# Moving the operand sums of the first product group ahead, next to the norm's operands, in a two-layer hybrid encoder

## The chip, the cores and the metric

The kernel runs on one core of one Trainium2 chip. The metric is device time in microseconds (us): the median of several executions of the whole program. One more execution is taken with the hardware profiler, and all views of the profile are of that one. The engines are called as in the profile: PE (matrix multiply) with PEld (its weight loads), DVE (vector), ACT (scalar and activation functions), POOL (GpSimd) and SP (which here only issues DMAs).

## The reference

The program is an encoder trunk of two layers on 256 tokens of width 1024, in float32. Per layer there are two SwiGLU blocks of inner width 2816 and an attention mixer between them; the edit concerns the SwiGLU blocks.

```
for l in range(DEPTH):
    x = x + 0.5 * swiglu(rms_norm(x, ffn1_norm[l]), ffn1_w_gate[l], ffn1_w_up[l], ffn1_w_down[l])
    h = rms_norm(x, mix_norm[l])
    ...                                   # projection, windowed and differential attention
    x = x + jnp.concatenate([out_a, out_b], axis=-1) @ w_out[l]
    x = x + 0.5 * swiglu(rms_norm(x, ffn2_norm[l]), ffn2_w_gate[l], ffn2_w_up[l], ffn2_w_down[l])
return rms_norm(x, final_norm)

def swiglu(h, w_gate, w_up, w_down):
    return (jax.nn.silu(h @ w_gate) * (h @ w_up)) @ w_down
```

## The kernel before

**Precision.** Every matrix is split into a high part, which ACT casts to the fast matmul type, and a low part, which DVE gets by subtracting the high part from the original. A product is three matmuls: high by high, low by high, high by low. So every weight of the network passes through ACT once (the cast) and DVE once (the subtraction). In the profile these are `CAST w<-raw` and `TENSOR_TENSOR w<-raw,w`, each on half of a raw tile (128x1024).

**Weights.** A raw tile is 1 MB of weights. There are six slots for raw tiles (`N_RAW`). SP loads a tile into a slot as soon as the slot's last reader, a subtraction on DVE, is done. `weights()` (line 249) hands out the next tile and calls `ahead` (line 228), which emits the splits in order, up to `look[0]` half tiles ahead of use. With `less` the call looks less far ahead.

**A SwiGLU block** (`ffn`, line 600) works through the inner width in groups of 512 columns, 0 to 4, and a rest of 256. Group 0 is computed plainly: gate and up (`gs`, `us`) over eight chunks of the inner dimension, in two passes of four (`tokens`). Then ACT computes the silu of the gate (`gate`, the activation `tmp<-ps,r`), and DVE multiplies it with up (`hidden`, the operation `s<-ps,hr,tmp`, one per token half). The hidden values are transposed by PE (`turn`, matmuls `ps<-ident,s`), split, and multiplied with the down weights in the next group.

**Groups of seven products.** For the groups in `SEVEN` gate and up are computed together by `by_seven` (line 632), a Strassen-like scheme: seven products of 512x512 weight quarters instead of eight. In the first block of layer 0 these are groups 2 to 4; in the other three blocks they are groups 1 to 4. Per group there are four raw tiles: a and d (quarters of gate), b and c (quarters of up). A DMA issued by POOL gathers c onto b (tile b+c), another gathers b onto a (tile a+b), and DVE adds c and then d to a+b. Products 1, 2 and 4 use quarters of the normalised input; products 3, 7, 5 and 6 use four sums of these quarters. In group 1 the order on PE is: product 1, transposes of the first half of group 0's hidden values, product 2, transposes of the second half, first down tile of group 0, products 3, 7, 5, 6, 4, second down tile.

**The sums.** `Norm.copies` (line 339) has ACT make plain float32 copies of the transposed input out of PSUM: eight activations `s<-ps,gcol`. `Norm.make_sums` (line 349) is a generator: its first step adds the first two sums on DVE (`tmp<-s,s`), the second casts them on ACT (`q<-tmp`), the third takes their low parts and adds the other two sums, the fourth casts those (`q<-tmp`, `v<-tmp`), and the fifth takes their low parts. The caller steps it with `next(sums)`.

**Order.** PE, ACT, DVE and POOL execute their instructions in the order in which they are written here: in the SwiGLU blocks that order is kept (`Kept`, line 40). Each engine runs its own list and waits for semaphores of the others. An instruction that waits holds up all that stand behind it on its engine. PSUM has eight banks; a product can start only when a bank has been read out.

**Norm statistics.** `before(1)` makes the operands of the last four chunks and the last squares; `before(2)` has DVE sum the squares (`ms<-nss`), POOL take the power (`r<-ms,mhalf`), DVE halve the result (`hr<-r`), and then lets waiting gathers go to POOL's queue (`flush`).

Of the kernel before, what the change touches and what calls it, by code (L numbers as in the profile page):

```python
# [29 lines left out]
IN_FFN, IN_MIX = 8, 6  # L30
# [4 lines left out]
def trunk(ctx: ExitStack, tc: tile.TileContext, x, n1, g1, u1, d1, nm, w_in, sink,  # L35
# [35 lines left out]
    def bank():  # L71
        return ps.tile([P, 512], F32, tag="ps", bufs=8, name=nm_("ps"))

    def halves(b):
        return b.rearrange("p (a n) -> p a n", a=2)

    def blk(dt=F32R):
        return s4.tile([P, 2, 512], dt, tag="s4", name=nm_("s4"))

    def tmp(tag="tmp", bufs=5, shape=(P, 2, 256), dt=F32):  # L80
        return tp.tile(list(shape), dt, tag=tag, bufs=bufs, name=nm_(tag))
# [143 lines left out]
    look = [IN_MIX]  # L225
# [23 lines left out]
    def weights(less=0, held=False):  # L249

        i = at["use"]
        at["use"] += 1
        if i > 1:
            ahead(2 * i + look[0] - less)
        w = loaded[i]
        w.held = held
        return w
# [179 lines left out]
    norm = Norm(0)  # L437
# [101 lines left out]
    def split(dst, src, scale=None):  # L539

        act.copy(dst[:, :, 0:S], src)
        dve.tensor_tensor(dst[:, :, S:512], src, f(dst[:, :, 0:S]), op=ALU.subtract)
# [57 lines left out]
    def ffn(norm, aside=None, before=None, final=False, sevens=SEVEN[1]):  # L600
        def silu(out_, acc, t):
            act.activation(out_, acc, AF.Silu, scale=norm.r[:, t:t + 1])
            return out_

        def gate(gs):
            g = []
            for t in range(2):
                n = gs[t].shape[1]
                g.append(silu(tmp().rearrange("p a n -> p (a n)")[:, :n], gs[t], t))
            return g  # L610

        def up(h, acc, g, t):
            n = acc.shape[1]
            dve.scalar_tensor_tensor(h[:, t, :n], in0=acc, scalar=norm.hr[:, t:t + 1], in1=g, op0=ALU.mult, op1=ALU.mult)

        def hidden(g, us):
            h = blk(F32)
            for t in range(2):
                up(h, us[t], g[t], t)
            return h  # L620

        def prod(xo, w):
            acc = bank()
            for k in range(4):
                hi, lo = w.part(k)
                xh, xl = xo(k)
                pe.matmul(acc, lhsT=xh, rhs=hi, start=k == 0, stop=False)
                pe.matmul(acc, lhsT=xl, rhs=hi, start=False, stop=False)
                pe.matmul(acc, lhsT=xh, rhs=lo, start=False, stop=k == 3)
            return acc  # L630

        def by_seven(h, g, sums):


            flat = lambda: tmp().rearrange("p a n -> p (a n)")

            def put(o, x, y, op):
                dve.tensor_tensor(o, x, y, op=op)
                return o

            m1, m7 = flat(), flat()
            if g > 1:
                act.copy(m1, prod(norm.quarter(0, 0), weights()))
                act.copy(m7, prod(norm.summed(3), weights(held=True)))
                hT = turn(h, 2)
                p2 = prod(norm.quarter(0, 1), weights())
                g0 = put(flat(), p2, m1, ALU.add)
                p3 = prod(norm.summed(2), weights())
                silu(g0, g0, 0)
                down(hT, g - 1, 0, weights())  # L650
            else:
                p1 = prod(norm.quarter(0, 0), weights(3, True))
                hT = turn(h, (0,))
                next(sums, None)
                w = weights(3, True)
                act.copy(m1, p1)
                p2 = prod(norm.quarter(0, 1), w)
                hT += turn(h, (1,))
                g0 = put(flat(), p2, m1, ALU.add)
                next(sums, None)  # L660
                silu(g0, g0, 0)
                down(hT, 0, 0, weights())
                p3 = prod(norm.summed(2), weights())
                act.copy(m7, prod(norm.summed(3), weights()))
            h = blk(F32)
            p5 = prod(norm.summed(0), weights())
            late = g == max(sevens)
            p6 = prod(norm.summed(1), weights(look[0] - 5 if late else 0, late))
            u2 = put(flat(), p6, m1, ALU.subtract)
            u3 = put(m7, m7, u2, ALU.add)  # L670
            p4 = prod(norm.quarter(1, 1), weights(look[0] - 4 if late else 0, late))
            g1 = put(m1, p4, u3, ALU.subtract)
            w = weights(look[0] - 3 if late else 0)
            silu(g1, g1, 1)
            put(u3, u3, p5, ALU.subtract)
            put(u2, u2, p5, ALU.subtract)
            put(u2, u2, p3, ALU.add)
            up(h, u2, g0, 0)
            up(h, u3, g1, 1)
            down(hT, g - 1, 1, w)  # L680
            return h

        def turn(hs, n):
            out_ = []
            for i in (range(n) if isinstance(n, int) else n):
                sl = halves(bank())
                for c in range(2):
                    for t in range(2):
                        pe.transpose(sl[:, c, t * P:(t + 1) * P], hs[:, t, (2 * i + c) * P:(2 * i + c + 1) * P], ident)
                hb = blk()  # L690
                split(hb, sl)
                out_.append(hb)
            return out_

        accs = [[bank(), bank()] for _ in range(2)]

        def down(hT, g, h, w):
            tokens(accs[h], [None] * (2 * g) + hT, w, 4 * g, last=(FC - 1, G4 - 1) if final and h else FC - 1)


        gs, us = [bank(), bank()], [bank(), bank()]
        if before is None:
            before = norm.late
        look[0] = IN_FFN - (1 in sevens)
        before(0)
        ws = (weights(), weights(2))
        for k in (0, 2):
            if k:
                before(1)
            for sl, w in zip((gs, us), ws):  # L710
                tokens(sl, norm.xs, w, 0, (k, k + 1))
        before(2)
        w = weights()
        sums = iter(())
        if 1 in sevens:
            norm.copies()
            sums = norm.make_sums()
            next(sums)
        tokens(gs, norm.xs, w, 4)
        if 1 in sevens:  # L720
            w = weights()
            g = gate(gs)
        else:
            g = gate(gs)
            w = weights()
        next(sums, None)
        tokens(us, norm.xs, w, 4)
        h = hidden(g, us)
        next(sums, None)
        for n in range(1, NGRP):  # L730
            if n in sevens:
                look[0] = IN_FFN + min(sevens) - n if before is not take_x else IN_MIX - (n == NGRP - 1)
                h = by_seven(h, n, sums)
                continue
            sums = norm.make_sums()
            gs = [bank(), bank()]
            tokens(gs, norm.xs, weights(), 0)
            hT = turn(h, 2)
            norm.copies()
            next(sums, None)  # L740
            tokens(gs, norm.xs, weights(), 4)
            g = gate(gs)
            next(sums, None)
            us = [bank(), bank()]
            for k0 in (0, 4):
                tokens(us, norm.xs, weights(), k0)
                next(sums, None)
            h = hidden(g, us)
            for hh in range(2):
                down(hT, n - 1, hh, weights())  # L750
                if hh == 0:
                    next(sums, None)

        gu = [bank(), bank()]
        tokens(gu, norm.xs, weights(), 0)
        hT = turn(h, 2)
        tokens(gu, norm.xs, weights(), 4)
        h = hidden(gate([b[:, 0:256] for b in gu]), [b[:, 256:512] for b in gu])

        def rest():  # L760
            hE = turn(h, 1)
            if aside is not None:
                aside()
            return hE
        return accs, hT, rest
# [294 lines left out]
    for l in range(DEPTH):  # L1060
# [7 lines left out]
        if not final:  # L1068
            norm = Norm((l + 1) * 8)
# [76 lines left out]
```

## Time and profile before

| what | value |
|---|---|
| median of 3 runs | 938.99 us (937.91 to 940.9) |
| the profiled execution | 939.61 us, its span 937.8 us |
| mean granted clock of PE | 0.997 |
| PE busy | 913.1 us (97%) |
| DVE busy | 807.4 us (86%) |
| ACT busy | 590.4 us (63%) |

The profiled execution took 939.61 us, of which the span is the time from the first to the last instruction. A row of the timeline gives start and length in us, engine, the line (here nearly always that of a helper), operation, tile written and tiles read, and how many instructions were merged. In square brackets stands how long the engine was idle before it, and what ended that. In the table by stretches the columns are: stretch, its length, then the busy time and in brackets the number of instructions of PE, PEld, DVE, ACT and POOL, the granted clock of PE (1 is full), the busy share of the DMA engines, and GB/s.

### The profile page before, as it was taken

How to read it: one execution, taken by the hardware profiler on the slowest of the kernel's cores; microseconds unless marked ns; L12 is line 12 of the kernel's file. 1: busy time of each engine (PE TensorE's matmuls, PEld its weight loads, DVE VectorE, ACT ScalarE, POOL GpSimd, SP SyncE). 2: the span in 40 equal slices, each digit the busy share in tenths (PEclk: the TensorE clock that was granted, in tenths of full speed). 3: DMA queues.
4: the chain of work that ended last, by engine and by line, in shares of the span. 5: the costliest groups of instructions: out<-in, count | busy, mean ns of one | idle time of the engine just before them, and what ended most of it. 6: DMA issues, size and time to landing. Idle time of an engine off the chain costs nothing.

```text
span 937.8 us, 12599 instructions
## 1 busy us (share of the span) xinstructions
PE 913.1 (97%) x4696; PEld 764.6 (82%) x4696; DVE 807.4 (86%) x1125; ACT 590.4 (63%) x917; POOL 66.9 (7%) x83
## 2 busy tenths in 40 slices
PE   7999999999999989999999899999999999899997
PEld 6888887899878868787888688888998888687886
DVE  6769999869866899999778999997698669999995
ACT  7836675567756676566575666665577485666661
POOL 0501000000001011000010010000001010010011
PEclk9999999999999999999999999999999999999999
DMA  9987897837255498897784998887462484998831
GB/s 338 355 217 216 241 262 268 254 97 234 91 180 140 131 298 247 231 265 259 269 205 133 266 271 229 244 287 229 114 222 91 137 201 136 280 265 233 243 143 46
DMA packets 114061, 200.87 MB, mean 214 GB/s; under 512 B 3662, under 2 KB 31376, under 8 KB 114000
## 3 DMA queue, kind: packets, MB, share of 16 engines
q1 hardware_dynamic: 96528, 166.74, 52.7%
q0 software_dynamic: 16096, 31.75, 18.8%
q10 hardware_dynamic: 1376, 1.57, 0.5%
q8 instruction: 37, 0.61, 0.3%
q14 instruction: 24, 0.20, 0.1%
HBM read 199.00 MB, written 1.05 MB: 213 GB/s over the span
## 4 chain that ended last, share of the span: by engine, by line
PE 56%; DVE 20%; DMA 12%; ACT 6%; issue 4%; POOLq 0%; ACTq 0%; POOL 0%; DVEq 0%
PE ps L50 56%; DVE w L50 12%; DMA raw<-in_ffn_w_up_dram 12%; ACT w L50 4%; DVE tmp L50 4%; DVE raw L50 2%; DVE s L50 2%; ACT s L50 1%; ACT tmp L50 1%; DMA xk<-in_x_dram 1%; ACT junk L50 0%; ACT q L50 0%; ACT L50 0%; DVE q L50 0%; ACT v L50 0%
## 5 line engine op out<-in xcount | busy, mean ns | idle before, releaser
L50 PE MATMUL ps<-w,s 128*128 128x512 f32 (+1 forms) x2574 | 604.1, 392 | 7.5 <-DVE tmp L50 5.6
L50 PEld LDWEIGHTS ps<-w,s 128*128 128x128 f32 x2574 | 478.3, 189 | 108.7 <-ACT w L50 6.9
L50 DVE TENSOR_TENSOR w<-raw,w 128x1024 fp32r<-128x1024 f32 (+1 forms) x458 | 483.3, 1101 | 44.2 <-ACT w L50 43.4
L50 ACT CAST w<-raw 128x1024 fp32r<-128x1024 f32 (+1 forms) x458 | 410.1, 952 | 134.5 <-DVE raw L50 91.8
L50 PE MATMUL ps<-w,q 128*128 128x512 f32 x540 | 127.3, 389 | 0.0
L50 PEld LDWEIGHTS ps<-w,q 128*128 128x128 f32 x540 | 101.4, 188 | 21.0
L50 PE MATMUL ps<-s,w 128*128 128x256 f32 x672 | 84.0, 285 | 0.0
L50 PEld LDWEIGHTS ps<-s,w 128*128 128x128 f32 x672 | 81.7, 191 | 1.1
L50 POOL DMA_DIRECT2D raw<-in_ffn_w_up_dram x30 | 38.9, 1296 | 494.0 <-DVE w L50 168.4
L50 DVE TENSOR_TENSOR raw<-raw,raw 128x1024 f32<-128x1024 f32 x60 | 70.6, 1219 | 0.0
L50 ACT ACTIVATE s<-ps,gcol 128x256 fp32r<-128x256 f32 (+1 forms) x80 | 31.3, 478 | 47.4 <-PE ps L50 45.7
L50 PE MATMUL ps<-ident,s 128*128 128x128 f32 x304 | 43.1, 276 | 4.3 <-DVE s L50 4.1
L50 ACT ACTIVATE tmp<-tmp,r 128x512 f32<-128x512 f32 x30 | 21.7, 722 | 39.8 <-DVE tmp L50 39.8
L50 PEld LDWEIGHTS ps<-ident,s 128*128 128x128 f32 x304 | 34.8, 140 | 14.2 <-DVE s L50 9.4
L50 ACT CAST s<-ps 128x512 fp32r<-128x512 f32 x44 | 24.2, 589 | 35.1 <-PE ps L50 34.9
L50 PE MATMUL ps<-w,v 128*128 128x512 f32 x180 | 43.5, 391 | 1.2 <-DVE tmp L50 1.2
L50 PEld LDWEIGHTS ps<-w,v 128*128 128x128 f32 x180 | 33.7, 188 | 9.0 <-issue 2.0
L50 ACT ACTIVATE s<-s,negm 128x256 f32<-128x256 f32 x64 | 31.9, 501 | 6.6 <-DVE negm L50 6.4
L50 DVE TENSOR_TENSOR tmp<-ps,tmp 128x512 f32<-128x512 f32 x49 | 33.5, 684 | 1.6 <-PE ps L50 1.6
L50 DVE SCALAR_TENSOR_TENSOR s<-ps,gcol,s 128x256 fp32r<-128x256 f32 x48 | 20.3, 478 | 15.5 <-ACT s L50 15.4
L50 DVE TENSOR_TENSOR s<-ps,s 128x512 fp32r<-128x512 f32 x44 | 28.7, 685 | 5.3 <-ACT s L50 5.3
L50 DVE TENSOR_TENSOR tmp<-tmp,ps 128x512 f32<-128x512 f32 x45 | 29.5, 683 | 0.5
(106 smaller groups left out, 398.3 us busy)
## 6 DMA issues: line engine op xcount, KB each, us to landing
raw<-in_ffn_w_down_dram SPq DMA_DIRECT2D x44, 1024.0 KB, 8.5
raw<-in_ffn_w_gate_dram SPq DMA_DIRECT2D x39, 1024.0 KB, 5.6
raw<-in_ffn_w_up_dram SPq DMA_DIRECT2D x39, 1024.0 KB, 5.2
raw<-in_ffn_w_up_dram POOLq DMA_DIRECT2D x30, 1024.0 KB, 11.8
raw<-in_w_in_dram SPq DMA_DIRECT2D x14, 1024.0 KB, 5.5
raw<-in_ffn_w_gate_dram SPq DMA_DIRECT2D x8, 512.0 KB, 6.8
raw<-in_ffn_w_up_dram SPq DMA_DIRECT2D x8, 512.0 KB, 7.7
raw<-in_w_in_dram SPq DMA_DIRECT2D x8, 512.0 KB, 5.7
```

What stands on the lines that cost most here:

```text
L50: ins = issue(*a, **k)
```

## The change

In blocks whose group 1 uses seven products, the copies are made directly behind the norm's last operands, between the two halves of group 0's first pass. The sums are then made in steps during group 0's second pass, all of them before `hidden`. The look-ahead is set to eight half tiles (`IN_FFN`) already at the last `weights()` of group 0, where it was seven until group 1. In group 1 the first two `weights()` calls look 0 and 1 half tiles less far ahead; before, it was 3 each. `by_seven` no longer steps the sums. The block without a seven-product group 1 keeps its order.

```diff
-        def by_seven(h, g, sums):
+        def by_seven(h, g):
...
-                p1 = prod(norm.quarter(0, 0), weights(3, True))
+                p1 = prod(norm.quarter(0, 0), weights(0, True))
                 hT = turn(h, (0,))
-                next(sums, None)
-                w = weights(3, True)
+                w = weights(1, True)
                 act.copy(m1, p1)
                 p2 = prod(norm.quarter(0, 1), w)
                 hT += turn(h, (1,))
                 g0 = put(flat(), p2, m1, ALU.add)
-                next(sums, None)
                 silu(g0, g0, 0)
...
         for k in (0, 2):
             if k:
                 before(1)
+                if 1 in sevens:
+                    norm.copies()
             for sl, w in zip((gs, us), ws):
                 tokens(sl, norm.xs, w, 0, (k, k + 1))
         before(2)
+        sums = norm.make_sums() if 1 in sevens else iter(())
+        next(sums, None)
         w = weights()
-        sums = iter(())
-        if 1 in sevens:
-            norm.copies()
-            sums = norm.make_sums()
-            next(sums)
+        next(sums, None)
         tokens(gs, norm.xs, w, 4)
         if 1 in sevens:
+            next(sums)
+            look[0] = IN_FFN
             w = weights()
+            next(sums)
             g = gate(gs)
+            next(sums)
         else:
             g = gate(gs)
             w = weights()
-        next(sums, None)
         tokens(us, norm.xs, w, 4)
         h = hidden(g, us)
-        next(sums, None)
         for n in range(1, NGRP):
             if n in sevens:
...
-                h = by_seven(h, n, sums)
+                h = by_seven(h, n)
```

The order in which PE, SP and POOL execute their instructions is the same in both kernels; ACT's and DVE's differ between the norm's operands and the split of tile a+b in group 1.

## The prediction

> **What bounds the kernel now.** I read the first lines of the page, then the busy time of each engine by stretch of time, then the timeline around the edited code.
>
> ```profile
> span 937.8 us, 12599 instructions
> PE 913.1 (97%) x4696; PEld 764.6 (82%) x4696; DVE 807.4 (86%) x1125; ACT 590.4 (63%) x917; POOL 66.9 (7%) x83
> ```
>
> By this PE bounds the kernel and DVE has 14% to spare. That average hides the stages that the edit touches. Three of the four SwiGLU blocks build group 1 from seven products. I call them B (second block of layer 0), C (first of layer 1) and D (second of layer 1). The first two rows below are block B's group 0 and its groups 1 to 4; the last two are groups 1 to 4 of C and D. Columns: span, then PE, PEld, DVE, ACT and POOL busy, granted clock, DMA share, GB/s.
>
> ```profile
> 297.15:320.15 23.00, 23.00 (x107) 19.03 (x106) 17.77 (x25) 17.56 (x28) 2.00 (x2) 1.00 0.64 142
> 320.15:431.33 111.18, 107.16 (x478) 86.88 (x476) 109.53 (x111) 70.74 (x81) 7.70 (x6) 1.00 0.87 246
> 501.60:614.16 112.56, 108.65 (x478) 88.19 (x476) 109.63 (x111) 70.63 (x81) 7.71 (x6) 0.98 0.85 243
> 782.97:894.63 111.66, 107.23 (x478) 86.86 (x476) 109.55 (x111) 70.79 (x81) 7.70 (x6) 1.00 0.86 245
> ```
>
> In groups 1 to 4 DVE is busy 109.6 us of 111 to 113, and PE waits for it. In group 0 it is the reverse: PE never stops, while DVE is idle 5.2 of 23.0 us. So a block ends when DVE ends, and DVE's dense stretch starts at the split of raw tile a+b, the third of four subtractions in the 320.15 row further down (about 322.4). Whatever moves that point moves the block's end, less the little idle time that DVE has behind it. Most of that sits at one place in each block, where the next group's b+c tile lands late:
>
> ```profile
> 338.03 4.84 ACT L50 CAST w<-raw 128x1024 fp32r<-128x1024 f32 x5 [0.93 <-DMA raw<-in_ffn_w_up_dram]
> 339.11 2.36 DVE L50 TENSOR_TENSOR w<-raw,w 128x1024 fp32r<-128x1024 f32 x2 [0.49 <-ACT w L50]
> 521.87 2.36 DVE L50 TENSOR_TENSOR w<-raw,w 128x1024 fp32r<-128x1024 f32 x2 [1.81 <-ACT w L50]
> 802.37 2.36 DVE L50 TENSOR_TENSOR w<-raw,w 128x1024 fp32r<-128x1024 f32 x2 [0.93 <-ACT w L50]
> 342.22 2.97 PE L50 MATMUL ps<-w,s 128*128 128x512 f32 x12 [1.27 <-DVE tmp L50]
> 524.98 4.58 PE L50 MATMUL ps<-w,s 128*128 128x512 f32 x12 [2.56 <-DVE tmp L50]
> 805.48 3.01 PE L50 MATMUL ps<-w,s 128*128 128x512 f32 x12 [1.75 <-DVE tmp L50]
> 431.33 5.05 PE L50 MATMUL ps<-w,s 128*128 128x512 f32 x21 [0.46 <-DVE w L50]
> ```
>
> DVE loses 0.49, 1.81 and 0.93 us there, 3.2 in all. PE's waits of 1.3, 2.6 and 1.8 us directly behind are longer because a bank of PSUM is freed by a DVE addition queued after those subtractions. At 431.33, where the block ends, PE again waits for DVE.
>
> **The change, part by part.** Nothing is added or removed, and PE's, SP's and POOL's own orders stay as they are. What moves is ACT's and DVE's order in group 0, and by the rows of block B it moves like this.
>
> ```profile
> 293.39 19.31 PE L50 MATMUL ps<-w,s 128*128 128x512 f32 x84
> 296.08 3.88 ACT L50 CAST w<-raw 128x1024 fp32r<-128x1024 f32 x4
> 299.87 3.01 ACT L50 ACTIVATE s<-ps,gcol 128x256 f32<-128x256 f32 x8
> 300.56 0.15 DVE L50 TENSOR_REDUCE ms<-nss 128x2 f32<-128x4 f32 x1
> 301.00 0.71 POOL L50 TENSOR_TENSOR r<-ms,mhalf 128x2 f32<-128x2 f32 x1 [8.23 <-DVE ms L50]
> 301.75 0.17 DVE L50 TENSOR_SCALAR hr<-r 128x2 f32<-128x2 f32 x1 [0.83 <-POOL r L50]
> 302.96 0.68 DVE L50 TENSOR_TENSOR tmp<-s,s 128x512 f32<-128x512 f32 x1
> 304.78 1.28 ACT L50 ACT_TABLE_LOAD   x1
> 306.07 1.27 ACT L50 ACTIVATE tmp<-ps,r 128x512 f32<-128x512 f32 x2
> 307.23 1.14 ACT L50 CAST q<-tmp 128x512 fp32r<-128x512 f32 x2
> 310.49 1.40 DVE L50 SCALAR_TENSOR_TENSOR s<-ps,hr,tmp 128x512 f32<-128x512 f32 x2
> 312.53 0.60 PE L50 MATMUL ps<-ident,s 128*128 128x128 f32 x4
> 312.89 3.00 PE L50 MATMUL ps<-w,s 128*128 128x512 f32 x12
> 316.37 0.59 ACT L50 CAST s<-ps 128x512 fp32r<-128x512 f32 x1
> 318.45 0.72 ACT L50 ACTIVATE tmp<-tmp,r 128x512 f32<-128x512 f32 x1 [1.50 <-DVE tmp L50]
> 320.15 4.63 DVE L50 TENSOR_TENSOR w<-raw,w 128x1024 fp32r<-128x1024 f32 x4 [0.59 <-ACT w L50]
> 322.54 0.37 SPq L153 DMA_DIRECT2D raw<-in_ffn_w_up_dram  x1
> ```
>
> Steps from these rows, start to start: a weight cast on ACT 0.95 us, a weight subtraction on DVE 1.13, the eight copies 2.9, a sum or a low part 0.60 (0.72 if it needs the one before), a gate 0.58, a half of hidden 0.66, a cast of a sum 0.6.
>
> The copies now start at 296.1, and the casts of a and d, which they used to follow, run from 298.9 to 302.7. That delay is harmless: PE needs a only behind the first 72 of the 84 matmuls, at about 309.9.
>
> The sums don't gain from it. The norm's statistics stand behind three subtractions on DVE (300.0 to 303.4), POOL's power follows, and hr, which DVE executes ahead of the sums, ends at 304.7 (301.9 before). The sums run from 304.7 to 306.0. POOL's gather of b onto a, queued behind the power, leaves about 3 us later; its tile is used over 15 us later, so this costs nothing. If that cover went, it would add to the same junction.
>
> ACT is idle from 302.7 to 305.4, waiting for the first sum. Then it casts two sums, both halves of group 0's first down tile and the first half of c, until 309.6. The two sums and that half of c stood behind the gates and are now ahead of them. The third and fourth sums follow on DVE behind a subtraction that waits for a cast; the fourth ends at 311.4. ACT casts it until 312.1, loads the silu table (1.28) and computes both gates, 313.4 to 314.6, against 306.1 to 307.3 before. The other half of c is cast until 315.6, DVE subtracts it until 316.8, and only then comes hidden, because it is queued behind that subtraction: both halves are ready at 318.2, against 311.9 in the trace.
>
> PE transposes hidden directly after product 1. In the trace it does so at 312.53, and hidden had been ready 0.6 us. Now PE stands still from 312.5 to 318.2, a **new wait of 5.7 us**. Block C loads no table at this place; only 0.9 of the 1.28 counts, since DVE then limits, and its wait is 4.8.
>
> The junction: DVE's second subtraction of b+c now ends at 321.6 instead of 322.5, so SP's load of the next b, which waits for it at 322.54, starts 0.9 us earlier (1.8 in C). That is what the edit gains. But product 2 now starts at 318.7 and ends at 321.4, the second transposes at 321.9, their copy out (0.59), low part (0.69), sum for the gate (0.68) and gate (0.72) end at 324.6, the cast of a+b (1.05) at 325.7. Its subtraction starts at 325.7 instead of 322.4: **3.2 us later** in B and D, 2.3 in C.
>
> From there the orders are as before. The late landing no longer holds DVE up, since DVE comes later and the data earlier: 0.5, 1.8 and 0.9 us go. The block ends move by 3.2 - 0.5 = 2.7, 2.3 - 1.8 = 0.5 and 3.2 - 0.9 = 2.3 us, 5.5 together. PE is not the limit behind the junction: the old waits in groups 1 to 4 (some 4.0 us of idle in the 320.15 window, and time lost in starting up again at each) give back most of the 5.7.
>
> The last term is the clock. After C's wait of 2.56 us the trace shows:
>
> ```profile
> 522.43:525.84 3.41, 0.86 (x4) 0.76 (x5) 3.38 (x5) 3.20 (x4) 0.00 (x0) 1.00 1.07 363
> 525.84:529.25 3.41, 3.41 (x10) 2.64 (x9) 3.41 (x4) 0.79 (x2) 0.00 (x0) 0.50 1.11 259
> 800.00:806.00 6.00, 4.25 (x19) 3.25 (x18) 5.04 (x7) 4.71 (x5) 1.28 (x1) 1.00 1.05 395
> ```
>
> PE was busy 0.86 of 3.41 us, and the next 3.41 us were granted at half clock, 1.7 us of lost matmul time; D's wait of 1.75 us went unpunished. Waits of 4.8 and 5.7 us are longer than C's, so I expect the half clock after each. It falls on product 2 and the transposes, that is on the path to the junction, for as much of it as is left when PE resumes. Bounds are 0 and 1.7 us per block; I take 1.2, since part of the slow stretch passes while PE still waits. Three blocks: 3.6 us. [...]
>
> Sum by the rows: 5.5 + 3.6 = +9.1 us on the profiled execution's 939.6, so 948.7. The median of the runs shown is 938.99, 0.6 lower, so the forecast is 948.1.
>
> **The rivals.** *No price for the clock.* The new waits come, but the slow stretch falls into the wait or behind product 2. For it: 1.75 us cost nothing in D. Against it: C's 2.56 did. 938.99 + 5.5 = 944.5. Chance 0.22.
>
> *Nothing given back.* The wait for hidden adds in full: 5.7 + 4.8 + 5.7 + 3.6 = 19.8, so 958.8. For it: PE is 97% busy overall. Against it: DVE's 109.6 busy us per block are there either way, and PE's old waits vanish behind the new one. It decides only if DVE falls idle again behind the junction. Chance 0.07.
>
> *Faster: the earlier b.* If hidden reaches PE before about 312.5 after all, because ACT and DVE interleave more tightly than I have read, only the earlier load is left. It can take away no more than DVE's 3.2 idle us: 938.99 - 3.2 = 935.8. For it: the b+c landing ends the longest PE wait in each block. Against it: the gates stand behind all four sums now, and the fourth alone comes out of DVE at 311.4. It decides if hidden is ready under 0.6 us late. Chance 0.07.
>
> *No difference.* Between these: hidden late by 2 to 3 us, taken back entirely at the b+c landing; 938 to 941. Chance 0.05.
>
> **How the numbers follow.** My forecast, new wait plus clock, has 0.59 and its own range of 945 to 951.5, from the clock term at 0.2 and 1.7 per block and 1 us of error in the junction. The range of 943 to 953.5 takes in the rival without the clock, and part of the way to nothing given back; it leaves out no more than two in ten. About 0.3%, 2.8 us, is what a measurement of this kernel can tell from no change. Faster by more: 0.07; within: 0.05; slower by more: 0.88.
>
> **What would show each step.** In the changed profile, block B's four transposes behind product 1 should start near 318 with a wait on DVE's s tile of 5 to 6 us, C's slightly shorter than D's; ACT's gates should stand some 7 us later against the norm's copies. The half clock should appear in three stretches soon after. The next b's load should leave 0.9 to 1.8 us earlier, and the waits at 342, 525 and 805 should be gone. I am wrong if the transposes wait under 2 us, or if DVE shows idle time behind the junction that it does not have now.

## The result, and the profile after

The changed kernel took 949.8 us in the median of 4 runs (949.26 to 953.57), the kernel before 939.6 beside it (937.91 to 940.9, 4 runs). The ratio is 1.0118, with a 95% interval of 1.0087 to 1.015: slower by 10 us. The profiled execution took 949.46 us. The first two lines of the page of the changed kernel:

```profile
span 947.7 us, 12604 instructions
PE 917.5 (97%) x4696; PEld 768.4 (81%) x4696; DVE 807.6 (85%) x1125; ACT 591.0 (62%) x917; POOL 65.6 (7%) x83
```

The instructions of PE, DVE, ACT and POOL are as many as before, and DVE's busy time is the same to 0.2 us. PE's busy time has grown by 4.4 us (913.1 before) with the same 4696 matmuls, so some of them ran slower. The timeline of the changed kernel around block B's first transposes, columns as before:

```profile
292.61 19.30 PE L50 MATMUL ps<-w,s 128*128 128x512 f32 x84
304.66 1.35 ACT L50 CAST q<-tmp 128x512 fp32r<-128x512 f32 x2 [2.58 <-DVE tmp L50]
311.30 1.28 ACT L50 ACT_TABLE_LOAD   x1
312.59 1.26 ACT L50 ACTIVATE tmp<-ps,r 128x512 f32<-128x512 f32 x2
315.97 1.40 DVE L50 SCALAR_TENSOR_TENSOR s<-ps,hr,tmp 128x512 f32<-128x512 f32 x2
316.77 0.47 PE L50 MATMUL ps<-ident,s 128*128 128x128 f32 x1 [4.86 <-DVE s L50]
317.43 0.90 PE L50 MATMUL ps<-ident,s 128*128 128x128 f32 x3 [0.18 <-DVE s L50]
317.98 4.32 PE L50 MATMUL ps<-w,s 128*128 128x512 f32 x12
321.18 0.37 SPq L153 DMA_DIRECT2D raw<-in_ffn_w_up_dram  x1
326.47 2.36 DVE L50 TENSOR_TENSOR w<-raw,w 128x1024 fp32r<-128x1024 f32 x2 [1.79 <-ACT w L50]
```

Group 0 starts 0.8 us earlier in this profile than in the one before (292.61 against 293.39), so all steps in B are taken from that start. (In the twelve profiles of this document it lies between 292.47 and 294.42 us.) ACT idles 2.58 us for the first sum, as the prediction read from the rows of before. The gates stand 19.98 us behind the start (12.68 before). PE then waits 4.86 us for the first half of hidden. Product 2 takes 4.32 us where it took 3.00. The junction is the 326.47 row, the split of a+b, and DVE is idle for 1.79 us ahead of it.

The same transposes in blocks C and D, first of the kernel before, then of the changed one:

```profile
494.05 0.60 PE L50 MATMUL ps<-ident,s 128*128 128x128 f32 x4
775.35 0.60 PE L50 MATMUL ps<-ident,s 128*128 128x128 f32 x4
```

```profile
501.74 0.47 PE L50 MATMUL ps<-ident,s 128*128 128x128 f32 x1 [4.10 <-DVE s L50]
502.40 0.90 PE L50 MATMUL ps<-ident,s 128*128 128x128 f32 x3 [0.18 <-DVE s L50]
785.67 0.48 PE L50 MATMUL ps<-ident,s 128*128 128x128 f32 x1 [4.93 <-DVE s L50]
786.33 0.90 PE L50 MATMUL ps<-ident,s 128*128 128x128 f32 x3 [0.18 <-DVE s L50]
```

Before, these transposes had no wait. After, it is 4.10 us in C, which loads no table, and 4.93 in D.

Behind the junction the busy time by stretch of the changed kernel, from the junction to the block's end in B, C and D (length, then PE, PEld, DVE, ACT, POOL, granted clock, DMA share, GB/s):

```profile
326.47:434.75 108.28, 106.69 (x478) 87.16 (x476) 107.15 (x109) 68.64 (x79) 7.70 (x6) 1.00 0.85 243
511.15:619.49 108.34, 106.66 (x479) 87.17 (x477) 107.15 (x109) 68.68 (x79) 7.70 (x6) 1.00 0.86 243
796.37:904.49 108.12, 106.61 (x479) 87.15 (x477) 107.12 (x109) 68.66 (x79) 6.82 (x6) 1.00 0.86 243
```

DVE is busy for all but 1.0 to 1.2 us of them. The blocks' ends in the timelines, of before (C and D) and of after (B, C and D):

```profile
614.16 1.20 PE L50 MATMUL ps<-w,s 128*128 128x512 f32 x4 [0.44 <-DVE w L50]
894.63 1.65 PE L50 MATMUL ps<-w,s 128*128 128x512 f32 x6 [0.45 <-DVE w L50]
```

```profile
434.75 1.43 PE L50 MATMUL ps<-w,s 128*128 128x512 f32 x5 [0.44 <-DVE w L50]
619.49 1.87 PE L50 MATMUL ps<-w,s 128*128 128x512 f32 x7 [0.46 <-DVE w L50]
904.49 1.88 PE L50 MATMUL ps<-w,s 128*128 128x512 f32 x7 [0.48 <-DVE w L50]
```

From B's start to its end it is 142.14 us (137.94 before), from there to C's end 184.74 (182.83), from there to D's end 285.00 (280.47). The three steps have grown by 4.2, 1.9 and 4.5 us, 10.6 in all; less the 0.8 of the earlier start this is the 9.9 between the two spans. From D's end to the end of the span it is 43.2 us in both.

The clock, in the changed kernel's stretches of 3.41 us (columns as above):

```profile
310.58:313.99 3.41, 1.33 (x6) 0.75 (x4) 3.41 (x5) 3.30 (x5) 0.00 (x0) 1.00 0.62 126
313.99:317.41 3.42, 0.47 (x1) 0.18 (x1) 2.70 (x5) 1.75 (x2) 0.00 (x0) 0.50 0.62 241
317.41:320.83 3.42, 3.40 (x10) 2.83 (x11) 2.68 (x3) 2.02 (x3) 0.00 (x0) 0.50 0.00 0
501.73:505.14 3.41, 3.21 (x9) 2.53 (x10) 2.68 (x4) 1.80 (x3) 0.00 (x0) 0.50 0.04 14
785.03:788.45 3.42, 2.60 (x8) 2.02 (x9) 2.94 (x4) 1.18 (x2) 0.00 (x0) 0.50 0.01 4
788.45:791.87 3.42, 3.42 (x10) 2.65 (x9) 1.36 (x2) 0.84 (x2) 0.00 (x0) 0.50 0.21 37
```

The half clock follows the new wait in every block, in B and D for two stretches in a row.

### The profile page after: what moved, and what is told of

Same layout as the page of the kernel before. It is cut to its first block, busy times and chain, and to the rows that moved or that the text cites. A ratio compares the mean times of both kernels' runs of the same rounds, so it can differ in the third digit from the quotient of the medians.

```text
span 947.7 us, 12604 instructions
## 1 busy us (share of the span) xinstructions
PE 917.5 (97%) x4696; PEld 768.4 (81%) x4696; DVE 807.6 (85%) x1125; ACT 591.0 (62%) x917; POOL 65.6 (7%) x83
## 4 chain that ended last, share of the span: by engine, by line
PE 51%; DVE 29%; issue 8%; DMA 6%; ACT 5%; POOL 0%; POOLq 0%; ACTq 0%; DVEq 0%
PE ps L50 51%; DVE w L50 17%; DMA raw<-in_ffn_w_up_dram 5%; DVE tmp L50 5%; DVE raw L50 4%; ACT w L50 3%; DVE s L50 2%; ACT s L50 1%; ACT tmp L50 1%; DVE q L50 0%; DMA xk<-in_x_dram 0%; ACT junk L50 0%; ACT L50 0%; POOL r L50 0%; POOL raw L50 0%
## 5 line engine op out<-in xcount | busy, mean ns | idle before, releaser
L50 PE MATMUL ps<-ident,s 128*128 128x128 f32 x304 | 45.2, 283 | 17.9 <-DVE s L50 17.7
```

The costliest lines, as they stand in the source:

```text
L50: ins = issue(*a, **k)
```

## The experiments

All times are medians beside runs of the kernel before on the same chip. Theory: the sums, made ahead of the gates, delay hidden and with it DVE's junction; the deeper look-ahead takes some of that back; the half clock adds to it. Rivals: the early copies cost time of their own; the look-ahead is what costs; the clock costs nothing.

**Look-ahead undone.** The changed kernel with

```diff
-                p1 = prod(norm.quarter(0, 0), weights(0, True))
+                p1 = prod(norm.quarter(0, 0), weights(3, True))
                 hT = turn(h, (0,))
-                w = weights(1, True)
+                w = weights(3, True)
...
-            look[0] = IN_FFN
```

> The changed kernel with its deeper look-ahead undone (seven half tiles until group 1, the first two calls in group 1 look three less far): copies and sums stay early. Theory (the early sums hold up gate and hidden; the deeper look-ahead only helps, as it splits b+c before the gate of group 1): the wait of 5 us for hidden stays in every block, and both halves of b+c are again split behind the first gate of group 1, 2.3 us more on DVE's path per block: slower than the changed kernel by 3 to 7 us, 953 to 957. Rival (the extra half of c ahead of gate and hidden makes the wait): the wait shrinks by 1 us of cast and 1.1 us of subtraction to about 3 us, faster than the changed kernel by 3 to 6 us, 944 to 947.

Measured: 959.76 us (957.83 to 960.4) against 939.07, ratio 1.0207 (1.0181 to 1.0233). The direction is the theory's, the size is above its range. The timeline at the junction, and the waits view:

```profile
327.46 4.63 DVE L50 TENSOR_TENSOR w<-raw,w 128x1024 fp32r<-128x1024 f32 x4 [1.79 <-ACT w L50]
```

```profile
PE ps L50 <- DVE tmp L50: 6.7, 5, 2.4
```

The 327.46 row holds four half tiles: b+c has fallen back behind group 1's gate, and a+b is the third of the four, 2.28 us into the row, at 329.7. From the start of group 0 that is 3.2 us later than in the changed kernel. The waits at the late b+c landing (sum, count, longest) are back as well; the expectation had left those out. The kernel before has 6.8 us in 5 waits in that row, and the changed kernel has no such row. So the look-ahead is not what costs: without it the early copies and sums cost 20.7 us, and with it 10.2.

**Look-ahead alone.** The kernel before, with only the look-ahead part:

```diff
-                p1 = prod(norm.quarter(0, 0), weights(3, True))
+                p1 = prod(norm.quarter(0, 0), weights(0, True))
                 hT = turn(h, (0,))
                 next(sums, None)
-                w = weights(3, True)
+                w = weights(1, True)
...
         if 1 in sevens:
+            look[0] = IN_FFN
             w = weights()
             g = gate(gs)
```

> The kernel before with the deeper look-ahead of the change alone: copies and sums stay where they were. Theory: hidden comes under 1 us late (one cast and one subtraction more ahead of it, most of it inside DVE's idle 2.7 us), PE waits under 0.5 us; both halves of b+c are split some 4 us earlier, so the next group's b+c tile lands early and DVE's idle 0.5, 1.8 and 0.9 us go, and the split of a+b comes about 1.3 us earlier per block: faster than the kernel before by 4 to 7 us, 932 to 936. Rival (the look-ahead is what costs in the change): a wait for hidden of over 2 us per block with the half clock behind it, slower by 3 to 6 us, 943 to 946.

Measured: 930.59 us (929.8 to 932.54), ratio 0.9903 (0.9881 to 0.9924). Below the expected range, that is faster by more than expected. A second run of it, on another chip:

> The look-ahead alone once more, on the same chip and against the same runs as the next kernel, to tell whether the early copies cost anything beside it: 930 to 931.5.

Measured: 931.77 (929.5 to 932.12), ratio 0.9913 (0.9899 to 0.9926). The gain holds. The timeline of the first:

```profile
317.29 0.37 SPq L153 DMA_DIRECT2D raw<-in_ffn_w_up_dram  x1
320.26 2.36 DVE L50 TENSOR_TENSOR w<-raw,w 128x1024 fp32r<-128x1024 f32 x2 [0.59 <-ACT w L50]
428.41 7.79 PE L50 MATMUL ps<-w,s 128*128 128x512 f32 x33 [0.47 <-DVE w L50]
498.69 2.36 DVE L50 TENSOR_TENSOR w<-raw,w 128x1024 fp32r<-128x1024 f32 x2 [0.59 <-ACT w L50]
776.58 2.36 DVE L50 TENSOR_TENSOR w<-raw,w 128x1024 fp32r<-128x1024 f32 x2 [0.59 <-ACT w L50]
```

This execution's block B starts 0.83 us earlier than in the profile of before. With that taken out, the load of b leaves 4.4 us earlier (317.29 against 322.54), since both halves of b+c are now split ahead of the junction, and the junction itself is 1.3 us earlier (320.26 against 322.43). In C it is 498.69 - 428.41 = 70.28 us behind B's end, against 503.88 - 431.33 = 72.55: 2.3 earlier. In D (776.58, behind C's end at 606.95) it is 1.5 earlier. So the gain has two parts, the earlier junction, 5.1 us in the three blocks, and the end of the late landing's idle time, the 3.2 us of the kernel before. The half clock appears in none of the three blocks; the mean granted clock of this execution is 0.999, against 0.997 before.

**Copies.** The kernel before, with only the copies moved:

```diff
             if k:
                 before(1)
+                if 1 in sevens:
+                    norm.copies()
...
-            norm.copies()
             sums = norm.make_sums()
```

> The kernel before with one part of the change: the eight copies stand directly behind the norm's last operands; the sums and the look-ahead stay as they were. Theory (the wait comes from the sums and weight casts ahead of the gate): DVE's 2.7 us of idle time ahead of the first subtraction of c take up the 2.9 us by which the casts of a and d move, hidden is ready as before; within 1 us of the kernel before in every block, 938 to 941. Rival (the copies ahead of the casts of a and d are themselves the cost, since norm statistics and hr now come 2.9 us later): hidden comes some 3 us late, PE waits about 2 us in each block, 943 to 946.

Measured: 939.16 us in 10 runs against 939.07, ratio 1.0004 (0.9987 to 1.0022). They cost nothing and bring nothing that this interval, 0.2% to either side, could show. The same copies with the look-ahead, that is the changed kernel with only the sums put back where they were:

> The changed kernel with the sums alone put back where the kernel before had them: copies stay directly behind the norm's operands, look-ahead stays deeper. Theory (only the early sums cost): no wait over 1 us for hidden, no half clock in the three blocks, and the time of the look-ahead alone: 929 to 934. Rival (copies and sums cost only together with the look-ahead, because all three crowd ACT ahead of the gate): the copies' 2.9 us of delay, hidden by idle time before, now show: 936 to 940.

Measured: 933.0 (932.2 to 934.4), ratio 0.9929 (0.9913 to 0.9946), within the range of the theory. Once more, beside the second run of the look-ahead alone:

> Look-ahead and early copies once more, beside the look-ahead alone. Theory (the copies' 2.9 us lie inside idle time, and the 2.4 us by which the first run was slower came from one load of b that took 7.7 instead of 5.7 us in the second block): within 1 us of the look-ahead alone. Rival (the copies delay the statistics by 2.9 us, and with the deeper look-ahead DVE has no idle time left ahead of hidden to take that up): 2 to 3 us slower than the look-ahead alone, with a wait for hidden of 0.5 us in all three blocks.

Measured: 932.9 (931.56 to 937.07), ratio 0.9934 (0.9916 to 0.9951), against 0.9913 for the look-ahead alone. The 1.1 us between them is a little more than the 1 us expected and within the intervals, so whether the early copies cost anything beside the deeper look-ahead stays open. Against this kernel the changed one differs by the place of the sums alone: 949.8 - 933.0 = 16.8 us is what that place costs (16.4 with each taken against its own runs of the kernel before).

**Two sums early.** The changed kernel, with the third to fifth step of the sums behind hidden:

```diff
-            next(sums)
             look[0] = IN_FFN
             w = weights()
-            next(sums)
             g = gate(gs)
-            next(sums)
...
         h = hidden(g, us)
+        for _ in range(3):
+            next(sums, None)
```

> The changed kernel with only the first two sums early (added and cast ahead of the gate); the third step and all behind it follow hidden. Theory: two chains make up the wait of 4.9 us for hidden. The first, ACT idle until the statistics let DVE make the first sum, plus two casts, is still there and gives a wait of about 3 us; the second, third and fourth sum and their casts, is gone. Time between the look-ahead alone and the change, 935 to 943, with a wait for hidden of 2.5 to 3.5 us in the first and third of the three blocks and 1.5 to 2.5 in the second. Rival (the third and fourth sums are the whole cost): wait under 1 us, 929 to 933.

Measured: 943.59 us (942.68 to 945.48) against 939.22, ratio 1.0048 (1.0033 to 1.0063). It is 0.6 us above the highest time expected. PE's wait for hidden in block B:

```profile
314.22 0.33 PE L50 MATMUL ps<-ident,s 128*128 128x128 f32 x1 [2.45 <-DVE s L50]
```

It is 2.45 us instead of 4.86; in C 1.08 (4.10) and in D 2.51 (4.93). So with the first two sums early, for which ACT stops in the changed kernel for 2.58 us, a quarter to half of the wait is there; the steps of the last two bring the rest. The expectation had 2.5 to 3.5 us in B and D and 1.5 to 2.5 in C, a little more. In time it is not a quarter to half: this kernel is 943.59 - 933.0 = 10.6 us behind the one with only the copies and the look-ahead, of the 16.8. The half clock follows here too, for one stretch in each block (the mean granted clock is 0.993, against 0.990 in the changed kernel), and the three steps that were moved behind hidden now all run on DVE ahead of the split that follows hidden. The run doesn't separate these.

**Clock held up.** The changed kernel, with 18 more matmuls of 128x512 between product 1 and the transposes of group 1. They write the bank that the transposes overwrite, so the computation is unchanged:

```diff
-                hT = turn(h, (0,))
+                hT = turn(h, (0,), 18)
...
-        def turn(hs, n):
+        def turn(hs, n, warm=0):
...
-                sl = halves(bank())
+                b = bank()
+                for _ in range(warm):
+                    xv = norm.xs[0][:, 0]
+                    pe.matmul(b, lhsT=xv[:, 0:P], rhs=xv, start=True, stop=True)
+                sl = halves(b)
```

> The changed kernel with 18 extra matmuls of 128x512 per block (about 4.1 us of PE work) between product 1 and the transposes, written to the bank that the transposes then overwrite: PE works through most of its new wait and the output doesn't depend on them. Theory with the clock's price (1.2 us a block and more where two slow stretches followed each other): no half clock near these places, the three blocks end 1.2 to 2.3 us earlier each, 944 to 946. Rival (DVE sets the block's end whatever PE's clock is): the same as the changed kernel, 949 to 950.5. If the extra matmuls overrun the wait, the transposes start later by as much.

Measured: 945.03 us (944.9 to 945.56), ratio 1.0054 (1.0036 to 1.0073), within the expected range. The timeline:

```profile
293.42 19.30 PE L50 MATMUL ps<-w,s 128*128 128x512 f32 x84
312.56 4.24 PE L50 MATMUL ps<-s 128*128 128x512 f32 x18
317.58 0.33 PE L50 MATMUL ps<-ident,s 128*128 128x128 f32 x1 [0.78 <-DVE s L50]
318.54 3.00 PE L50 MATMUL ps<-w,s 128*128 128x512 f32 x12
325.71 2.36 DVE L50 TENSOR_TENSOR w<-raw,w 128x1024 fp32r<-128x1024 f32 x2 [1.79 <-ACT w L50]
433.81 2.55 PE L50 MATMUL ps<-w,s 128*128 128x512 f32 x10 [0.46 <-DVE w L50]
508.89 2.36 DVE L50 TENSOR_TENSOR w<-raw,w 128x1024 fp32r<-128x1024 f32 x2 [1.79 <-ACT w L50]
617.08 5.29 PE L50 MATMUL ps<-w,s 128*128 128x512 f32 x22 [0.44 <-DVE w L50]
791.46 2.36 DVE L50 TENSOR_TENSOR w<-raw,w 128x1024 fp32r<-128x1024 f32 x2 [1.79 <-ACT w L50]
900.62 5.73 PE L50 MATMUL ps<-w,s 128*128 128x512 f32 x24 [0.45 <-DVE w L50]
```

The added matmuls end at 316.80, ahead of the transposes, which come at the same time as in the changed kernel (24.16 us behind the start of group 0 in both). Product 2 takes 3.00 us again, and no stretch of these blocks has the half clock (the mean granted clock is 0.998, against 0.990). So the wait is kept and the clock's price is taken out. Block by block, from start to end, it is 140.39 us in B (142.14 in the changed kernel), 183.27 in C (184.74) and 283.54 in D (285.00): 1.75, 1.5 and 1.5 less, 4.7 in all. By the medians it is 949.8 - 945.03 = 4.8, or 4.2 with each taken against its own runs of the kernel before. In D of this execution it is 109.16 us from the junction to the block's end (900.62 - 791.46), 1.0 more than in the changed kernel (108.12), where B and C agree within 0.2; D's gain may be too small by that much. The rival, by which the clock costs nothing, falls. What stays, 6.0 us over the kernel before, is the price of the wait, less what the look-ahead gives back.

**The table.** The changed kernel, with the silu table loaded ahead of the block's work, by a Silu of one column that nobody reads:

```diff
         look[0] = IN_FFN - (1 in sevens)
+        if 1 in sevens:
+            act.activation(tmp("early", 1, (P, 1)), mhalf[:, 0:1], AF.Silu)
```

> The changed kernel with the silu table loaded early in the three blocks, as in the run with the look-ahead and the early table. Theory: 0.9 of the 1.28 us counted in the wait for hidden, so the waits of the first and third block become as long as the second's (about 4.1 instead of 4.9 us) and the blocks end about 0.9 us earlier: 947.5 to 948.5. If the shorter wait also spares one of the two slow clock stretches behind it, up to 1.7 us more per block: down to 944.5. Rival (ACT's load is hidden behind DVE's queue): no change, 949 to 950.5.

Measured: 947.58 us (946.99 to 948.99) against 938.77, ratio 1.009 (1.0077 to 1.0104), within the expected range. The wait in block B:

```profile
315.90 0.33 PE L50 MATMUL ps<-ident,s 128*128 128x128 f32 x1 [4.06 <-DVE s L50]
```

It is 0.8 us shorter (4.86), and about the same now as in C and D (4.12 and 4.13). That confirms the step by which 0.9 of the table's 1.28 us counted in the wait. The time gained is not the table's alone, though. The half clock now lasts one stretch in each block (mean granted clock 0.993), where it was two in B and D (0.990). In B it is the second of these rows, and the next stretch is at full clock:

```profile
313.66:317.07 3.41, 0.84 (x5) 0.65 (x6) 3.41 (x5) 0.61 (x1) 0.00 (x0) 1.00 0.73 276
317.07:320.48 3.41, 3.41 (x10) 2.63 (x9) 2.49 (x3) 2.02 (x3) 0.00 (x0) 0.50 0.00 0
```

Block by block, from start to end, B is 0.7 us shorter than in the changed kernel and D 1.9, and C, which loads no table in either, is 0.2 longer. In the changed kernel's rows the load from 311.30 takes 1.28 us, and the gates start at 312.59, directly where it ends.

**Look-ahead and table.** Since the look-ahead alone was faster than the kernel before, and the table is loaded there as well, the last version has both on the kernel before, and no early sums:

> The kernel before with the deeper look-ahead alone, and the silu table loaded early: an activation of one column, written to a scrap tile, at the start of each of the three blocks while ACT waits for PE, so that no load of 1.28 us stands ahead of the gates in the first and third block. Theory: with the look-ahead alone DVE still idles 2.5 us in the first block just before the first subtraction that waits for the gate's side of ACT; 1.3 us of that goes, the rest of the path to the split of a+b is set by PE's product 2, so it brings 0.5 to 2 us over the look-ahead alone: 928.5 to 930. Rival (PE's products alone set that path): no difference from the look-ahead alone, 930.6 within 0.7.

Measured: 928.61 us (927.6 to 929.67) against 939.22, ratio 0.9886 (0.9871 to 0.99), within the expected range. This is the fastest of all the kernels here, 10.6 us below the kernel before. DVE's subtraction ahead of hidden, first in the look-ahead alone, then with the table early:

```profile
309.45 1.23 DVE L50 TENSOR_TENSOR w<-raw,w 128x1024 fp32r<-128x1024 f32 x1 [2.51 <-ACT w L50]
```

```profile
309.47 1.23 DVE L50 TENSOR_TENSOR w<-raw,w 128x1024 fp32r<-128x1024 f32 x1 [1.12 <-ACT w L50]
```

DVE idles 1.4 us less. The two weren't run on the same chip, so the 2.0 us between their medians is less certain than each one's gain. The blocks of the two profiles agree with the theory: B is 1.0 us shorter with the table early, D 0.6, and C, which loads no table, 0.2.

## Why the prediction was right

**What bounds it.** Right. The block ends in C and D, as in B, are PE's waits for DVE (0.44 to 0.48 us), and behind the junction DVE is busy 107.1 of 108.1 to 108.3 us. In the kernel with the added matmuls PE does 18 more of them in each block, and the time goes down.

**The wait for hidden.** Right in cause, and right in size where it counts. The wait itself, 4.86 us, is a little under the 5 to 6 that the prediction named as a sign, because PE starts on the first half of hidden, 0.66 us ahead of the second; the prediction had it wait for both. Counted to the second half, from the start of group 0, the transposes stand at 24.82 us in the changed kernel (317.43 - 292.61); before, where all four run without a wait, they begin at 19.14: 5.7 later, as forecast. In C, counted from the end of B, it is 67.65 against 62.72, 4.9 later (forecast 4.8); in D, from the end of C, 166.84 against 161.19, 5.7 (forecast 5.7).

**The earlier b.** 0.6 us in B (321.18 and the 0.8 of the earlier start against 322.54) and 1.3 in C, where 0.9 and 1.8 were forecast. The landing no longer held DVE up in either, so the 0.3 and 0.5 us cost nothing there.

**The junction.** With the clock held up it is 32.29 us behind the start of group 0 in B (29.04 before), 75.08 behind the end of B in C (72.55) and 174.38 behind the end of C in D (171.09): 3.3, 2.5 and 3.3 later, forecast 3.2, 2.3 and 3.2. With the half clock, in the changed kernel, it is 4.8, 3.9 and 5.8.

**What is given back.** From the junction to the block's end it is 108.28, 108.34 and 108.12 us; before it was 108.90, 110.28 and 109.38, with the junction 2.28 us into the rows 320.15, 501.60 and 782.97. So 0.6, 1.9 and 1.3 were given back, where the late landing's idle time of 0.5, 1.8 and 0.9 was forecast. PE's waits for DVE's tmp are gone, as expected.

**The clock.** This is the term that was too small. I took 1.2 us per block, 3.6 in all; 4.7 went by the blocks when the clock was held up. At the junction, by the figures just given, the half clock adds 1.6 us in B, 1.3 in C and 2.5 in D. C, with one slow stretch, is close to the 1.2 that I took. In B and D a second slow stretch followed, which the prediction didn't have, and D lies above its upper bound of 1.7. The reason given for less than 1.7, that part of the slow stretch passes while PE waits, holds for the first of the two in B and D, in which PE was busy 0.47 and 2.60 of 3.42 us, and hardly for C's (3.21 of 3.41).

**The sum.** +9.1 us forecast, 9.9 in the spans and 10.2 in the medians. By the blocks it is 10.6: 6.0 for the wait, where 5.5 was forecast, and 4.7 for the clock, where 3.6 was. That the spans differ by only 9.9 comes from the 0.8 us by which block B started earlier in this execution, which no term of the forecast has. So the clock's term was too small, and the nearness of 9.9 to 9.1 is in part luck. Whether the wait's term was too small as well is open, since the 6.0 holds the 1.0 us by which D of that execution is longer behind the junction.

**The rivals.** *No price for the clock* gave 5.5 us; the kernel without the half clock is at 6.0 over the kernel before, so that rival's price was about right and its condition failed. *Nothing given back* fell by the rows of the junction. *Faster: the earlier b* would have been at most 3.2 us by its text. That bound was wrong: the look-ahead alone, which has that effect without the wait, gained 8.5 us by the medians, and 7.0 in its repeat. The bound counted DVE's idle time behind the junction, and left out that the look-ahead moves the junction itself, by 1.3 us in B, 2.3 in C and 1.5 in D. In the sum the same effect was in the junction's own working, so the forecast didn't suffer.

So the change is two changes of opposite sign. The look-ahead is worth 7.0 to 8.5 us alone and 10.0 with the early sums (959.76 - 949.8); the place of the sums costs 16.8 with the deeper look-ahead and, together with the copies, 20.7 without it. These are differences of medians, in part from different chips.

## What to carry to other kernels

Work that is moved ahead on an engine that executes in order is paid for by whatever it is put in front of (16.8 us here for the sums), unless that had time to spare, as it had for the copies alone (939.16 us against 939.07). Ask which instruction stood at that place, whose result another engine needs next, and what the moved work itself has to wait for. Read an engine's idle time by stage and not from its average; 14% to spare on DVE was 1% behind the junction. And when an edit has several parts, try them alone: the part that looked like an accessory was worth 1%, and the main one cost twice as much.

## What the runs showed of the hardware that was not expected

In the profiles of the kernel before and of the changed one the granted clock changes in fixed stretches of 3.413 us. In the changed kernel the half clock begins at 313.99 us in B and at 785.03 in D, 138 of these stretches apart (471.04 us), and it lasts two, one and two of them in B, C and D (6.83, 3.41 and 6.83 us); only the one at 945.46 is cut off, by the end of the program. Before, it lasts one in C, from 525.84 to 529.25. The stretch ahead of the half clock was wholly idle on PE in C and D of the changed kernel, but not in B (1.33 of 3.41 us busy), nor in C before (0.86). Three more rows show the edge: in the first, of the kernel before, PE was busy 1.66 of 3.41 us, and no half clock followed; in the next two, of the kernel with two early sums, 1.79 us were followed by it.

```profile
802.32:805.73 3.41, 1.66 (x8) 1.11 (x7) 3.33 (x4) 3.41 (x5) 0.70 (x1) 1.00 1.05 397
```

```profile
500.57:503.98 3.41, 1.79 (x9) 1.09 (x8) 3.12 (x4) 3.36 (x6) 0.00 (x0) 1.00 0.00 0
503.98:507.39 3.41, 3.41 (x9) 2.67 (x8) 1.73 (x3) 1.65 (x3) 0.00 (x0) 0.50 0.49 130
```

Full-clock stretches with PE busy 0.84 us (the 313.66 row of the changed kernel with the early table), 0.86 (the 522.43 row of the kernel before), 1.20 (the stretch at 338.97 of the kernel with only the copies moved) and 1.33 (the 310.58 row of the changed kernel) were followed by half clock too, and one with 1.51 (at 500.37 in the changed kernel with its look-ahead undone) was not. With full clock behind 1.51 and 1.66 us and half clock behind 1.79, the share of busy time alone doesn't decide it; what else does stays open. In the last pair no single wait was long: the timeline of that kernel has two of under 0.9 us, and these are all of PE's idle time in the stretch:

```profile
502.06 0.49 PE L50 MATMUL ps<-w,s 128*128 128x512 f32 x1 [0.74 <-ACT s L50]
503.44 6.87 PE L50 MATMUL ps<-w,s 128*128 128x512 f32 x22 [0.88 <-DVE s L50]
```

The price can also be more than one stretch: at half clock, in the changed kernel, stretches with PE busy 0.47 us (the 313.99 row) and 2.60 us (785.03) were followed by another slow one, and those with 3.21 (501.73), 3.40 (317.41) and 3.42 us (788.45) by the full clock. Eighteen matmuls without a use in each of the three blocks, in a wait that was there anyway, brought back 4.2 to 4.8 us by the medians.
